# Narrowing stages: operand sums on VectorE in place, two pairs of k at a time, instead of GpSimd

## The chip, the cores and the metric

One core of one Trainium2 chip. The time is that of one execution of the program on the device, in microseconds (us), and a kernel's time is the median of its runs.

## What is computed

The reference runs two transformer blocks over a sequence of 512 tokens of width 1024 in fp32. Three times it ends a layer with a feed-forward network whose hidden width is 2816: a wide product, a gate, and a narrow product back to 1024 columns. The change touches only this last product.

```python
def swiglu(x, w_gate, w_up, w_down):
    return (jax.nn.silu(x @ w_gate) * (x @ w_up)) @ w_down

def _conv_ffn(x, w_in, conv_w, conv_b, w_out):
    u = x @ w_in
    up = jnp.pad(u, ((0, 0), (CONV_WIDTH_2 - 1, 0), (0, 0)))
    u = sum(conv_w[j] * up[:, j:j + s] for j in range(CONV_WIDTH_2)) + conv_b
    g, val = u[..., :D_FF_2], u[..., D_FF_2:]
    return (jax.nn.silu(g) * val) @ w_out
```

## The kernel before

An fp32 product is made of three TensorE products of rounded parts: ScalarE rounds an operand to its high part (`hh` of an activation, `wh` of a weight), VectorE subtracts to get the low part (`hl`, `wl`, line 185), and `mm3` (lines 436 to 438) multiplies high by high, high by low and low by high. Every weight piece that TensorE uses thus needs one VectorE subtraction of 1024 elements, and every activation operand one of 512.

The hidden activations lie in `hT`, 128 partitions by 22 k by 512 tokens. `down` makes the narrow product with seven block products in place of eight (a Strassen-like scheme): token halves `t` and `u`, pairs of k (`a1 = hT[:, 2g]`, `a2 = hT[:, 2g+1]`, eleven g), and halves of the columns. It has three stages, one after the other on TensorE:

- Stage 1 (`fetch1`, `pair`): four products per g into the banks R, Q, W, V, of `a1` (with its half u replaced by a1u - a2u, line 821) and `a2`. At its end R, Q, W and V are added to the residual `X` on VectorE (`end1` to `end4`: line 975 in block 1, line 1016 in the two convolution layers, then line 848).
- Stage 2 (`fetch2`): two products per g, of the sums that line 908 (VectorE) and line 909 (GpSimd, through `pool`, so the profile shows line 176) write into `hT`.
- Stage 3 (`third`): one product, of `s3 + s2`, which line 932 makes on GpSimd (again line 176), for two g at once, except the first.

In the profile's names an addition `hT<-hT` on GpSimd is one of line 909 (128x256) or of line 932 (128x512). The same queue of GpSimd also holds `biases`, line 422: four additions of a row to two tiles of `X`, 128x1024, which come once in each of the two convolution layers, and the multiplication `hT<-hT,tv` of `conv_ffn`, the last of the wide stage. `gains`, line 411, is VectorE's multiplication of `X` by a row. The layers are called layer 0 (`block1_ffn`), layer 1 (`conv_ffn(0)`) and layer 2 (`conv_ffn(1)`, the end of the program).

TensorE's order is written by hand. On the other engines a scheduler sets the order when the program is built; weight conversions run ahead of TensorE by a few pieces, and the sums of stages 2 and 3 are placed well ahead of use, most of them inside stage 1. Each engine then executes its own list strictly in order.

Of the kernel before, what the change touches and what calls it, by code (L numbers as in the profile page):

```python
# [16 lines left out]
ALU = mybir.AluOpType  # L17
# [5 lines left out]
S = 512  # L23
# [4 lines left out]
NF = D_FF // P  # L28
# [44 lines left out]
class Half:  # L73
# [6 lines left out]
    def fetch(self, j):  # L80
        if j in self.ops:
            return
        if j % 2 == 0:
            pc = self.net.piece()
            for e in range(2):
                c = slice(e * 512, (e + 1) * 512)
                self.pieces[j + e] = (pc[0][:, c], pc[1][:, c])
        self.ops[j] = self.lhs(self.order[j])
# [11 lines left out]
class Net:  # L100
# [699 lines left out]
    def operand(self, src, negative=False):  # L800

        self.operands += 1
        hp = self.hp[0 if self.operands % 8 in (1, 2) else 1]
        h = hp.tile([P, S], F32R, name="hh", tag="hh")
        l = hp.tile([P, S], F32R, name="hl", tag="hl")
        w = math.prod(src.shape[1:])
        view = lambda x: x[:, :w] if len(src.shape) == 2 else x[:, :w].rearrange("p (a b) -> p a b", b=256)
        if negative:
            self.nc.scalar.activation(view(h), src, AF.Copy, scale=-1.0)
            last = self.nc.vector.scalar_tensor_tensor(view(l), src, -1.0, view(h).bitcast(F32), op0=ALU.mult, op1=ALU.subtract)  # L810
        else:
            _, last = self.split(view(h), view(l), src)
        if 12 < self.operands <= 12 + NT:
            self.gains(last)
        return h, l
# [8 lines left out]
    def down(self, es, hT, first, done, last=False):  # L824

        nc, G = self.nc, NF // 2
        self.hp.append(es.enter_context(self.tc.tile_pool(name="hp", bufs=6, reuse_waits="tile")))
        t, u = slice(0, 256), slice(256, 512)  # L830
        TT = nc.vector.tensor_tensor
        bank = lambda pool, tag: [pool.tile([P, 512], F32, name="dn", tag=tag) for _ in range(2)]
        R, W, Q, V = bank(self.wk, "wk"), bank(self.wk, "wk"), bank(self.acc, "acc"), bank(self.acc, "acc")
        on = dict(skip_group_check=True)
        operand = self.operand

        def mms(ps, a, ca, b, cb, start, stop, tiles=(0, 1), **kw):

            for i in tiles:
                c, d = slice(256 * ca + i * P, 256 * ca + i * P + P), slice(512 * cb, 512 * cb + 512)  # L840
                self.mm3(ps[i], (a[0][:, c], a[1][:, c]), (b[0][:, d], b[1][:, d]), start, stop, **kw)

        def add(i, half, ps, op=ALU.add, begin=False):
            x = self.X[:, i, 512 * half:512 * half + 512]
            if begin:
                first(x, ps, op)
            else:
                TT(x, x, ps, op=op)  # L848

        def run(fetch, products, tail, wait=False):  # L850


            ops = []
            for g in range(G):
                while len(ops) < min(G, g + 1 + FETCH):
                    ops.append(fetch(len(ops)))
                if g < G - tail:
                    for f in products:
                        if wait and f is products[-1] and g < 2:
                            if g:  # L860
                                f(0, *ops[0])
                                f(1, *ops[1])
                        else:
                            f(g, *ops[g])
            for f in products:
                for g in range(G - tail, G):
                    f(g, *ops[g])
                f(None)

        def product(ps, a, ca, b, cb, begin, then):  # L870
            kw = {} if begin else on
            def f(g, *ops):
                if g is None:
                    then()
                else:
                    mms(ps, ops[a], ca, ops[b], cb, begin and g == 0, g == G - 1, **kw)
            return f


        def fetch1(g):  # L880
            if g + 1 < G:
                self.ahead.append(self.pair(hT, g + 1))
            return *self.ahead.pop(0), self.piece(), self.piece()

        def end1():
            for i in (0, 1):
                add(i, 0, R[i], begin=True)

        def end2():
            for i in (0, 1):  # L890
                add(i, 0, W[i])

        def end3():
            for i in (0, 1):
                add(2 + i, 1, Q[i], begin=True)

        def end4():
            for i in (0, 1):
                add(2 + i, 0, V[i], begin=True)

        self.boost = 0
        run(fetch1, [product(R, 0, 0, 2, 0, True, end1), product(Q, 0, 1, 3, 0, True, end3),
                     product(W, 1, 0, 2, 1, True, end2), product(V, 1, 1, 3, 1, True, end4)], 1, True)


        def fetch2(g):
            a1, a2 = hT[:, 2 * g, :], hT[:, 2 * g + 1, :]
            TT(a1[:, u], a1[:, u], a1[:, t], op=ALU.subtract)  # L908
            self.pool(a1[:, t], a2[:, t], a1[:, u], op=ALU.add)
            return operand(a1), self.piece()  # L910

        def end5():
            for i in (0, 1):
                add(i, 1, R[i], ALU.subtract, True)

        def end6():
            for i in (0, 1):
                add(i, 1, Q[i])
                done(i)

        self.pinned.enter_context(self.tc.manual_schedule(engines={mybir.EngineType.PE}))
        self.biases()
        run(fetch2, [product(R, 0, 1, 1, 0, False, end5), product(Q, 0, 0, 1, 1, False, end6)], 2)


        ops, tail = {}, 8 if last else 5

        def third(g):
            if g not in ops:
                m = 2 if g else 1  # L930
                s2, s3 = hT[:, 2 * g:2 * g + 2 * m:2, u], hT[:, 2 * g + 1:2 * g + 2 * m:2, u]
                self.pool(s3, s3, s2, op=ALU.add)
                x, w = operand(s3, True), self.piece()
                ops.update({g + e: (x, e, w, e) for e in range(m)})
            return ops[g]

        for g in range(G - tail):
            mms(R, *third(g), False, False, **on)
        for g in range(G - tail, G):
            third(g)  # L940
        if not last:
            self.new_xt()
        for i in (0, 1):
            if self.turns:
                self.turn(n=1)
            for g in range(G - tail, G):
                mms(R, *ops[g], False, g == G - 1, (i,), **on)
            for half in (0, 1):
                add(2 + i, half, R[i], (ALU.add, ALU.subtract)[half])
            done(2 + i)  # L950
# [609 lines left out]
```

## Time and profile before

| what | value |
|---|---|
| time, median of 3 runs (lowest to highest) | 1791.72 us (1788.81 to 1791.89) |
| time of the profiled execution | 1794.33 us |
| its span, first to last instruction | 1792.4 us |
| TensorE clock granted, mean | 0.975 of full speed |
| busy share: TensorE matmul, VectorE, ScalarE, GpSimd | 94%, 81%, 56%, 47% |

The rows further down come from the profiled execution, whose time is 2.6 us above the median of the runs. A busy share is a mean over the whole program; what counts here is which engine waits in the three narrowing stages, about 417 to 526 us, 1040 to 1160 us and 1664 to 1790 us.

### The profile page before, as it was taken

How to read it: one execution, taken by the hardware profiler on the slowest of the kernel's cores; microseconds unless marked ns; L12 is line 12 of the kernel's file. 1: busy time of each engine (PE TensorE's matmuls, PEld its weight loads, DVE VectorE, ACT ScalarE, POOL GpSimd, SP SyncE). 2: the span in 40 equal slices, each digit the busy share in tenths (PEclk: the TensorE clock that was granted, in tenths of full speed). 3: DMA queues.
4: the chain of work that ended last, by engine and by line, in shares of the span. 5: the costliest groups of instructions: out<-in, count | busy, mean ns of one | idle time of the engine just before them, and what ended most of it. 6: DMA issues, size and time to landing. Idle time of an engine off the chain costs nothing. (4 is left out here: it accounts for less than half of the span.)

```text
span 1792.4 us, 28144 instructions
## 1 busy us (share of the span) xinstructions
PE 1680.9 (94%) x10432; PEld 1490.2 (83%) x10432; DVE 1446.4 (81%) x2177; ACT 1008.8 (56%) x1733; POOL 850.0 (47%) x588
## 2 busy tenths in 40 slices
PE   7978999999999899999999997999998999999987
PEld 6856999998777788878999985887776889999865
DVE  6984676778885788977998899855888679888998
ACT  6663344545553587745665563644667555665652
POOL 2484733334235465217555546244232175655761
PEclk9988999999999999999999998999999999999998
DMA  6469566668876665744576688697442336666643
GB/s 230 168 187 254 158 152 193 176 190 308 319 223 174 162 165 146 202 108 137 162 192 176 183 297 292 197 243 190 115 119 81 99 108 158 188 173 185 202 153 112
DMA packets 106072, 326.05 MB, mean 182 GB/s; under 512 B 9888, under 2 KB 10016, under 8 KB 93904
## 3 DMA queue, kind: packets, MB, share of 16 engines
q1 hardware_dynamic: 73088, 215.53, 35.3%
q0 software_dynamic: 25648, 73.54, 21.8%
q10 hardware_dynamic: 7200, 35.20, 5.5%
q8 instruction: 82, 1.34, 0.3%
q14 instruction: 54, 0.44, 0.1%
HBM read 274.91 MB, written 73.43 MB: 194 GB/s over the span
## 5 line engine op out<-in xcount | busy, mean ns | idle before, releaser
L183 ACT ACTIVATE wh<-raw 128x1024 fp32r<-128x1024 f32 x457 | 450.6, 997 | 406.9 <-PE c L437 93.9
L185 DVE TENSOR_TENSOR wl<-raw,wh 128x1024 fp32r<-128x1024 f32 (+1 forms) x415 | 536.9, 1309 | 145.9 <-ACT wh L183 141.8
L176 POOL TENSOR_TENSOR raw<-raw 128x512 f32<-128x512 f32 x124 | 188.0, 1516 | 254.5 <-DMA raw<-raw 205.9
L436 PE MATMUL c<-xh,wh 128*128 128x256 f32 x992 | 284.4, 287 | 11.4 <-ACT m L519 10.3
L437 PE MATMUL c<-xl,wh 128*128 128x256 f32 x992 | 283.0, 285 | 0.0
L438 PE MATMUL c<-xh,wl 128*128 128x256 f32 x992 | 282.2, 284 | 0.0
L436 PEld LDWEIGHTS c<-xh,wh 128*128 128x128 f32 x992 | 191.0, 193 | 14.1 <-ACT m L519 12.4
L438 PE MATMUL dn<-wh,hl 128*128 128x512 f32 x462 | 182.0, 395 | 13.1 <-DVE hl L185 13.1
L437 PE MATMUL dn<-wl,hh 128*128 128x512 f32 x462 | 183.5, 398 | 9.0 <-DVE wl L185 8.9
L437 PEld LDWEIGHTS c<-xl,wh 128*128 128x128 f32 x992 | 191.2, 193 | 0.1
L438 PEld LDWEIGHTS c<-xh,wl 128*128 128x128 f32 x992 | 191.2, 193 | 0.0
L176 POOL TENSOR_TENSOR hT<-hT 128x256 f32<-128x256 f32 (+2 forms) x66 | 151.3, 2317 | 68.1 <-DVE hT L908 68.0
L436 PE MATMUL dn<-wh,hh 128*128 128x512 f32 x462 | 180.0, 395 | 0.0
L176 POOL TENSOR_TENSOR wl<-raw,wh 128x1024 fp32r<-128x1024 f32 (+1 forms) x42 | 95.8, 2286 | 87.0 <-ACT wh L183 83.0
L436 PE MATMUL fa<-xh,wh 128*128 128x256 f32 (+1 forms) x400 | 133.2, 333 | 1.7 <-ACT wh L183 1.7
L437 PE MATMUL fa<-xl,wh 128*128 128x256 f32 (+1 forms) x400 | 132.7, 332 | 1.1 <-DVE xl L185 1.1
L438 PE MATMUL fa<-xh,wl 128*128 128x256 f32 (+1 forms) x400 | 132.7, 332 | 0.8 <-DVE rs_t L326 0.8
L176 POOL TENSOR_TENSOR rs_r<-rs_t,mhalf 128x1 f32<-128x1 f32 (+1 forms) x40 | 32.4, 810 | 189.8 <-DVE rs_t L326 188.2
L437 PEld LDWEIGHTS dn<-wl,hh 128*128 128x128 f32 x462 | 88.1, 191 | 33.8 <-DVE wl L185 15.7
L438 PEld LDWEIGHTS dn<-wh,hl 128*128 128x128 f32 x462 | 88.1, 191 | 32.0 <-DVE hl L185 13.9
L150 POOL COPY paced<-wh 128x1 f32<-128x1 f32 x48 | 38.3, 798 | 154.3 <-ACT wh L183 154.1
L436 PEld LDWEIGHTS dn<-wh,hh 128*128 128x128 f32 x462 | 88.0, 191 | 18.4
(303 smaller groups left out, 4618.6 us busy)
## 6 DMA issues: line engine op xcount, KB each, us to landing
raw<-in_w_conv_dram SPq DMA_DIRECT2D x36, 1024.0 KB, 4.9
mixed<-in_narrow_dram ACTq DMA_DIRECT2D x48, 704.0 KB, 6.2
raw<-raw POOLq DMA_DIRECT2D x62, 512.0 KB, 5.1
raw<-mixed SPq DMA_DIRECT2D x51, 512.0 KB, 6.1
raw<-in_narrow_dram SPq DMA_DIRECT2D x48, 512.0 KB, 4.9
raw<-in_w_ffn_dram SPq DMA_DIRECT2D x18, 1024.0 KB, 4.9
mixed<-in_narrow_dram POOLq DMA_DIRECT2D x24, 704.0 KB, 10.1
mixed<-mixed POOLq DMA_DIRECT2D x24, 704.0 KB, 10.2
```

Source lines behind the costliest of these rows:

```text
L150: paced = self.nc.gpsimd.tensor_copy(m, self.ready[-1][0][:, 0:1].bitcast(F32))
L176: self.pooled = self.nc.gpsimd.tensor_tensor(*args, **kw)
L183: self.copied = self.nc.scalar.activation(hi, src, AF.Copy)
L185: return self.copied, sub(lo, src, hi.bitcast(F32), op=ALU.subtract)
L436: mm(ps, lh, rh, start=first, stop=False)
L437: mm(ps, lh, rl, start=False, stop=False)
L438: mm(ps, ll, rh, start=False, stop=last)
```

## The change

The 17 GpSimd additions of a layer go to VectorE. `fetch2` works on every second call only, for two pairs of k together: one subtraction and one addition of 128x2x256, and the addition is now written over `a2` half t, where before it was written over `a1` half t. The operand is then a contiguous run of 512 that begins in the middle of `a1`, so that its two halves change places, and the two products swap the number of the half that they read. `third` keeps its shape and changes engine.

```diff
+        flat = hT.rearrange("p k s -> p (k s)")
+
         def fetch2(g):
-            a1, a2 = hT[:, 2 * g, :], hT[:, 2 * g + 1, :]
-            TT(a1[:, u], a1[:, u], a1[:, t], op=ALU.subtract)
-            self.pool(a1[:, t], a2[:, t], a1[:, u], op=ALU.add)
-            return operand(a1), self.piece()
+            if g % 2 == 0:
+                a1, a2 = (hT[:, 2 * g + e:min(2 * g + 4, NF):2, :] for e in range(2))
+                TT(a1[:, :, u], a1[:, :, u], a1[:, :, t], op=ALU.subtract)
+                TT(a2[:, :, t], a2[:, :, t], a1[:, :, u], op=ALU.add)
+            return operand(flat[:, 2 * g * S + 256:2 * g * S + 768]), self.piece()
...
-        run(fetch2, [product(R, 0, 1, 1, 0, False, end5), product(Q, 0, 0, 1, 1, False, end6)], 2)
+        run(fetch2, [product(R, 0, 0, 1, 0, False, end5), product(Q, 0, 1, 1, 1, False, end6)], 2)
...
-                self.pool(s3, s3, s2, op=ALU.add)
+                TT(s3, s3, s2, op=ALU.add)
```

In the changed kernel the lines behind the diff have moved by three: 908 is 911, 909 is 912, 932 is 935, and 1016 is 1019.

GpSimd's list in layer 1, from the last multiplications of the wide stage to the three later additions of `biases` (line 422); before (-) there are sums of `hT` in between:

```order
+L176 TENSOR_TENSOR hT<-hT,tv 128x512 x3
 L422 TENSOR_TENSOR X<-X,row 128x2x512
-L176 TENSOR_TENSOR hT<-hT 128x256
-L176 TENSOR_TENSOR hT<-hT 128x2x256
-L176 TENSOR_TENSOR hT<-hT 128x256 x2
-L176 TENSOR_TENSOR hT<-hT 128x2x256
-L176 TENSOR_TENSOR hT<-hT 128x256 x2
-L176 TENSOR_TENSOR hT<-hT 128x2x256
 L319 DMA row<-in_rows_dram 128x1024
 L422 TENSOR_TENSOR X<-X,row 128x2x512 x3
```

Nothing of the sums is left on GpSimd, and the three additions of line 422 have only the row's load ahead of them.

VectorE's list in layer 1 where stage 1 ends and `X` is updated, before the change:

```order
L185 TENSOR_TENSOR wl<-raw,wh 128x1024
L1016 SCALAR_TENSOR_TENSOR X<-X,dn 128x512 x4
L185 TENSOR_TENSOR wl<-raw,wh 128x1024 x2
L848 TENSOR_TENSOR X<-X,dn 128x512 x2
L1016 SCALAR_TENSOR_TENSOR X<-X,dn 128x512 x2
L185 TENSOR_TENSOR hl<-hT,hh 128x512
```

The same place after it, with the last sums of the stage ahead of it:

```order
L912 TENSOR_TENSOR hT<-hT 128x2x256
L911 TENSOR_TENSOR hT<-hT 128x256
L935 TENSOR_TENSOR hT<-hT 128x2x256
L912 TENSOR_TENSOR hT<-hT 128x256
L185 TENSOR_TENSOR wl<-raw,wh 128x1024
L1019 SCALAR_TENSOR_TENSOR X<-X,dn 128x512 x3
L185 TENSOR_TENSOR wl<-raw,wh 128x1024 x2
L1019 SCALAR_TENSOR_TENSOR X<-X,dn 128x512
L848 TENSOR_TENSOR X<-X,dn 128x512 x2
L1019 SCALAR_TENSOR_TENSOR X<-X,dn 128x512 x2
L185 TENSOR_TENSOR hl<-hT,hh 128x512
```

The first operand of stage 2 (`hl`) still stands behind all eight instructions on `X`; the fourth of line 1016 has moved behind two weight conversions.

VectorE's list in layer 2 in the middle of stage 2, a piece of the difference:

```order
+L185 TENSOR_TENSOR hl<-hT,hh 128x512
 L810 SCALAR_TENSOR_TENSOR hl<-hT,hh 128x256
+L935 TENSOR_TENSOR hT<-hT 128x2x256
+L185 TENSOR_TENSOR wl<-raw,wh 128x1024
 L810 SCALAR_TENSOR_TENSOR hl<-hT,hh 128x512
+L935 TENSOR_TENSOR hT<-hT 128x2x256 x2
+L185 TENSOR_TENSOR wl<-raw,wh 128x1024
+L810 SCALAR_TENSOR_TENSOR hl<-hT,hh 128x512 x2
+L935 TENSOR_TENSOR hT<-hT 128x2x256
+L185 TENSOR_TENSOR wl<-raw,wh 128x1024
+L935 TENSOR_TENSOR hT<-hT 128x2x256
```

In layer 2 five of the six sums of stage 3 and one narrow one of stage 2 now come between the operands of stages 2 and 3, behind the end of stage 1.

## Rows read from the trace of the kernel before

**Rows 1.** The page's busy times: busy us, share of the span, instructions.

```profile
PE 1680.9 (94%) x10432; PEld 1490.2 (83%) x10432; DVE 1446.4 (81%) x2177; ACT 1008.8 (56%) x1733; POOL 850.0 (47%) x588
```

**Rows 2.** Busy time by stretch: stage 1 of layers 1, 2; then transition, stages 2-3.

```profile
core 0: us, PE busy (x) PEld busy (x) DVE busy (x) ACT busy (x) POOL busy (x), PEclk, DMA share, GB/s
1040.00:1104.00 64.00, 61.32 (x265) 49.01 (x265) 62.16 (x74) 36.36 (x47) 37.63 (x18) 1.00 0.91 317
1104.00:1120.00 16.00, 5.77 (x16) 4.25 (x15) 15.23 (x12) 2.37 (x4) 10.59 (x7) 0.68 0.69 246
1664.00:1730.00 66.00, 59.91 (x248) 46.77 (x247) 65.86 (x74) 36.84 (x49) 47.03 (x19) 0.97 0.51 167
1730.00:1779.00 49.00, 48.74 (x213) 39.38 (x212) 47.88 (x56) 22.26 (x27) 16.43 (x8) 1.00 0.40 134
```

**Rows 3.** Waits of TensorE, layers 0, 1, 2: us in total, times, longest.

```profile
PE dn L438 <- DVE hl L185: 2.9, 1, 2.9
...
PE dn L438 <- DVE hl L185: 10.2, 1, 10.2
PE dn L437 <- DVE wl L185: 2.5, 3, 1.9
...
PE dn L437 <- DVE wl L185: 6.4, 8, 2.1
```

**Rows 4.** Timeline, layer 1, end of stage 1: start, us, instruction [idle before, releaser].

```profile
1099.22 2.73 DVE L1016 SCALAR_TENSOR_TENSOR X<-X,dn 128x512 f32<-128x512 f32 x4 [1.84 <-PE dn L438]
1101.86 3.50 DVE L185 TENSOR_TENSOR wl<-raw,wh 128x1024 fp32r<-128x1024 f32 x2
...
1107.07 6.94 POOL L422 TENSOR_TENSOR X<-X,row 128x1024 f32<-128x1024 f32 x3
...
1107.67 6.90 DVE L185 TENSOR_TENSOR hl<-hT,hh 128x512 fp32r<-128x512 f32 x1
...
1114.62 0.79 PE L438 MATMUL dn<-wh,hl 128*128 128x512 f32 x1 [10.23 <-DVE hl L185]
```

**Rows 5.** VectorE by shape, 1664 to 1730: count | busy us, mean ns | idle.

```profile
L185 DVE TENSOR_TENSOR wl<-raw,wh 128x1024 fp32r<-128x1024 f32 x21 | 30.0, 1440 | 0.1
L185 DVE TENSOR_TENSOR hl<-hT,hh 128x512 fp32r<-128x512 f32 x25 | 23.0, 938 | 0.0
L411 DVE TENSOR_TENSOR X<-X,row 128x1024 f32<-128x1024 f32 x4 | 6.5, 1624 | 0.0
L821 DVE TENSOR_TENSOR hT<-hT 128x256 f32<-128x256 f32 x9 | 4.7, 534 | 0.0
```

**Rows 6.** The same in layer 1, 1040 to 1104.

```profile
L185 DVE TENSOR_TENSOR wl<-raw,wh 128x1024 fp32r<-128x1024 f32 x22 | 32.4, 1489 | 0.0
L185 DVE TENSOR_TENSOR hl<-hT,hh 128x512 fp32r<-128x512 f32 x20 | 15.8, 816 | 0.0
```

**Rows 7.** The same in layer 0, 482 to 500, with no sum on GpSimd.

```profile
L185 DVE TENSOR_TENSOR wl<-raw,wh 128x1024 fp32r<-128x1024 f32 x7 | 8.6, 1224 | 3.4 <-ACT wh L183 3.4
L185 DVE TENSOR_TENSOR hl<-hT,hh 128x512 fp32r<-128x512 f32 x10 | 6.5, 684 | 0.0
```

**Rows 8.** Timeline, layer 1, VectorE and GpSimd together.

```profile
1086.33 1.29 DVE L185 TENSOR_TENSOR hl<-hT,hh 128x512 fp32r<-128x512 f32 x2
1087.54 0.41 DVE L908 TENSOR_TENSOR hT<-hT 128x256 f32<-128x256 f32 x1
1087.87 1.22 DVE L185 TENSOR_TENSOR wl<-raw,wh 128x1024 fp32r<-128x1024 f32 x1
...
1086.55 19.94 POOL L176 TENSOR_TENSOR hT<-hT 128x256 f32<-128x256 f32 x8 [9.12 <-DVE hT L908]
```

**Rows 9.** Timeline, layer 2: GpSimd's first row, then VectorE's waits.

```profile
1669.70 5.16 POOL L176 TENSOR_TENSOR hT<-hT,tv 128x512 f32<-128x512 f32 x1 [4.58 <-ACT hh L183]
...
1652.41 1.23 DVE L185 TENSOR_TENSOR wl<-raw,wh 128x1024 fp32r<-128x1024 f32 x1 [1.93 <-ACT wh L183]
...
1763.75 0.69 DVE L848 TENSOR_TENSOR X<-X,dn 128x512 f32<-128x512 f32 x1 [0.89 <-PE dn L438]
```

**Rows 10.** The chain that ended last: its first row, and the last on VectorE.

```profile
1771.30 3.40 DVE X L383 x2
...
1787.69 0.75 DVE X L384
```

## The prediction

> **What bounds the kernel now.** I read the page's busy shares first, then the busy times of the narrowing stages, then what TensorE waits for there, then the durations of VectorE's instructions by shape, and last the timelines at the longest waits. TensorE is busy 94% of the span and VectorE 81% [rows 1], so the share alone says TensorE. By stage it reads otherwise: in stage 1 of layer 2 VectorE is busy 65.9 of 66 us while TensorE works 59.9, and in stage 1 of layer 1 it is 62.2 of 64 [rows 2]. All waits of TensorE in these stages are for VectorE, for `wl` or `hl`: 2.9 us in layer 0, 12.7 in layer 1, 6.4 in layer 2 [rows 3]. That is 22.0 us, the most that a faster supply of operands can take out of the waits themselves.
>
> VectorE is slow there because GpSimd stands in its way. With no sum on GpSimd `wl` takes 1224 ns and `hl` 684 [rows 7]; in layer 2 they mean 1440 and 938 [rows 5], in layer 1 1489 and 816 [rows 6]. The longest single wait shows the mechanism: an `hl` of 684 ns lasts 6.90 us, just as long as three additions of line 422 run on GpSimd, and TensorE idles 10.2 us for it [rows 4]. Both have two inputs in SBUF. An addition of line 422 takes 2.31 us there (6.94/3), and VectorE does nothing meanwhile. From 1652.4 us VectorE has no wait but 0.89 us until the end [rows 9], and the chain that ended last is VectorE's from 1771 to the end [rows 10]. So in layer 2 VectorE's work sets the end, in layer 1 TensorE waits at the end of stage 1, and in layer 0 TensorE loses 2.9 us once.
>
> The blocking isn't one-sided. From 1086.6 to 1106.4 eight sums on GpSimd take 19.94 us, while `hl` and `wl` beside them run at 1.29 for two and 1.22 [rows 8]: here GpSimd waited and VectorE paid nothing. The Trainium skill ("SBUF — State Buffer", Who interferes with whom) says that whichever of the two starts first has the shared pair for the whole instruction and the other fully blocks; the 6.90 us agree, but by the rule alone VectorE would pay for most sums. If it paid for all, at half of line 422's 2.31 us for a 512 and a quarter for a 256, a layer's 6 and 11 sums would hold it 13.3 us, and layer 2 would gain 13.3 - 6.7 + 0.9 = 7.5 us in place of the 4.3 worked out below. I use the stretch of the rows.
>
> **The change, part by part.**
>
> Removed from VectorE: eleven subtractions of line 908 a layer. One takes 0.33 us from its start to the next [rows 8], so 3.7 us.
>
> Added to VectorE: in each of lines 911, 912 and 935 five additions of 512 elements and one of 256, so 15 and 3. The trace has no 2x256 addition on VectorE; the nearest row is `hl`, 128x512, two of which take 1.29 us, so 0.60 each when the next overlaps its end, and 0.68 alone [rows 7, 8]. Line 912 reads what 911 has just written, so I take 0.68 for its five, 0.60 for the other ten, 0.33 for the three narrow ones: 3.4 + 6.0 + 1.0 = 10.4 us. The net is +6.7 us a layer. Ends: 10.0 if all overlap, 11.2 if none do.
>
> Given back to VectorE: the stretch. In layer 2 against the undisturbed times (1224 ns standing for the 1024-wide line 411 too) [rows 5, 7, 8]: `wl` 21 x 0.216 = 4.5, `hl` 25 x 0.254 = 6.4, line 411 4 x 0.40 = 1.6, line 821 9 x 0.12 = 1.1, together 13.6 us. Not all of it is the sums': one line 422 (2.3 us) and the long multiplication `hT<-hT,tv` (5.16 us mostly waiting [rows 9]; as a 512, half of a line 422, about 1.2) stay. 10.1 us go. In layer 1 [rows 6, 7]: 22 x 0.265 + 20 x 0.132 = 8.5 us, less the same 3.5, so 5.0. In layer 0 TensorE doesn't wait inside stage 1, so nothing there counts.
>
> On the path, layer by layer:
>
> *Layer 2.* VectorE is the bound from end to end, so its work counts: 6.7 - 10.1 = -3.4 us, and the added sums fill its idle 0.9 us at 1763.8 [rows 9], so **-4.3**. TensorE can follow: its 6.4 us of waits and the half-speed clock after them (0.97 mean over 66 us [rows 2], some 2 us) leave it 8. The order matters here: 5 of the wide sums stand behind the end of stage 1 and delay the final normalization, which is why TensorE's 8 us are not the gain.
>
> *Layer 1.* Up to the end of stage 1 VectorE gets 5.8 net (10 subtractions go; 912 five wide, 911 five, 935 three, and three narrow: 3.4 + 4.8 + 1.0 - 3.4) and 5.0 back; its wait of 1.84 for TensorE [rows 4] covers the rest. Of the 2.5 us of waits for `wl` half should go, because the stretch lies ahead of line 422 and many of the sums behind it: **-1.2**. Then the 10.2 us. GpSimd's list before holds the eight sums of rows 8 until 1106.4, so line 422 began at 1107.07; its first input is ready when the fourth line 1016 ends. In the new order that is after three of them, two `wl` of 1.2 without the stretch that makes them 3.50 now, and one more: 1099.2 + 1.9 + 2.3 + 0.7 = 1104.1. The `hl` behind it still waits for all three additions, and TensorE for it, but 2.9 us sooner: **-2.9**. Should `hl` slip in between the first and second addition, the second `hl` meets the others, so the gain stays near 3 to 4 us.
>
> *Layer 0.* The 2.9 us wait is an `hl` that stands behind eight additions to `X` which wait for TensorE; that order stays: **0**.
>
> The sum is -4.3 - 1.2 - 2.9 = -8.4 us. The profiled execution would go from 1794.3 to 1785.9; against the median of the runs, 2.6 us below it, 1791.7 - 8.4 = **1783 us**.
>
> Nothing new waits for ScalarE: each sum on VectorE stands behind the `hl` of the same pair, which had already waited for ScalarE's read. GpSimd loses 17 sums a layer; it idles.
>
> **The rivals.**
>
> *The relief is larger (0.09).* If the `hl` after stage 1 of layer 1 misses line 422 altogether, the 10.2 us wait falls to what layer 0 has, 2.9, and the 2 us at half clock behind it (0.68 over 16 us [rows 2]) shrink too. For it: GpSimd starts earlier. Against: three additions of 2.31 us still follow the same update of `X`. With it -8.4 - 6 = 1777; with all of layer 1's waits gone 1772.
>
> *No change (0.21).* VectorE's relief equals its new work: at 11.2 us for the sums and the stretch given back only two thirds (6.7 in layer 2), layer 2 gains nothing, and layer 1 gives 0 to 3: 1788 to 1794, about 1790. For it: rows 8, where sums cost VectorE nothing, so that its stretch may be owed to other work on GpSimd.
>
> *Slower (0.13).* VectorE, which had no gap in layer 2, now has 6.7 us more to do, and line 422 on GpSimd, freed of the sums ahead of it, comes earlier and takes the port at a moment when TensorE has no operand in hand. The point where it decides is in layer 2: if less than 5.8 of the 10.1 us come back (6.7 less the idle 0.9), it is longer than before. At a quarter back, layer 2 costs 6.7 - 2.5 - 0.9 = +3.3, and in layer 1 5.8 - 1.3 - 1.8 = +2.7 more wait ahead of line 422: +6, 1798. Against it: the stretch in rows 5 is measured, and GpSimd has nothing else there. A rule speaks for it: the Trainium skill ("Perfetto Trace Analysis", Optimizing Scalar/DVE Operations) advises to move work to GpSimd where VectorE is saturated, and adds that the shared read port may undo it; the second half is what rows 4 to 6 show.
>
> **How the numbers follow.** My forecast has 0.57, the larger relief 0.09, no change 0.21, slower 0.13. The likeliest case by itself is 1778 to 1788: the sums between 10.0 and 11.2 a layer, the stretch of layer 2 between 8 and 13.6, the transition between 0 and 4 us. Runs of this kernel lie within 3 us of each other, so 0.2% (3.6 us) is about what can be told from no change. Faster by more than that takes in the first two cases, 0.66; within it 0.21; slower 0.13. The range reaches up to cover no change and down to the larger relief: 1773 to 1793 leaves out about the slow case and the tail of the other.
>
> **What would show it.** Right: no `hT<-hT` of 128x256 or 128x512 on GpSimd; lines 911, 912 and 935 near 0.68 us for 512 elements; `wl` in stage 1 of layer 2 near 1.28 us and `hl` near 0.75; the waits of TensorE for `wl` in layer 2 down from 6.4 us to under 2; the long wait of layer 1 ending within about 12 us of the end of R's products instead of 15. Wrong: `wl` and `hl` as long as before, so GpSimd's sums were not what stretched them; a new wait of TensorE before 1104 us in layer 1 as long as the old; or, in layer 2, TensorE freed but the final normalization as late as before, which would say that the sums placed behind stage 1 took everything back.

## The result and the profile after

The changed kernel takes 1782.1 us (median of 4 executions, 1780.6 to 1783.6) where the kernel before took 1791.8 beside it: a ratio of 0.9937, 95% interval 0.9921 to 0.9953. With more executions on another chip it was 0.9950 (0.9931 to 0.9969). The prediction was 1783.0.

The busy times of the page after, in the columns of [rows 1]:

```profile
PE 1673.8 (94%) x10432; PEld 1485.5 (83%) x10432; DVE 1445.4 (81%) x2198; ACT 1008.7 (57%) x1733; POOL 779.9 (44%) x537
```

VectorE's total is the same within 1 us of [rows 1], though it makes all the sums now; GpSimd's is 70 us less. The busy times by stretch, which answer to the second and third row of [rows 2] (the second stretch, like that of before, ends 0.9 us ahead of the first update of `X`; the first begins 0.9 us ahead of it, where that of before began 4.8 behind it):

```profile
1097.00:1113.00 16.00, 11.58 (x39) 8.51 (x38) 15.08 (x13) 6.83 (x9) 11.30 (x6) 0.79 0.81 312
1649.00:1715.00 66.00, 65.07 (x313) 54.50 (x314) 65.95 (x89) 42.82 (x60) 23.54 (x4) 1.00 0.62 205
```

In 66 us of stage 1 of layer 2 TensorE now works 65.1 us instead of 59.9, at a granted clock of 1.00, which is the 2.4 GHz level, instead of a mean of 0.97. In the 16 us of layer 1's transition it works 11.6 instead of 5.8, and 11.4 in the 16 us that begin 4.8 us behind the first update. VectorE is as full as before in both. TensorE's waits in layers 1 (two rows) and 2 (one), against [rows 3]:

```profile
PE dn L438 <- DVE hl L185: 4.6, 2, 4.0
PE dn L437 <- DVE wl L185: 0.5, 1, 0.5
...
PE dn L437 <- DVE wl L185: 1.9, 3, 1.0
```

With the 3.0 of layer 0, which stayed, 22.0 us of waits are now 10.0. VectorE's durations by shape in layer 2, 1649 to 1715, against [rows 5]:

```profile
L185 DVE TENSOR_TENSOR wl<-raw,wh 128x1024 fp32r<-128x1024 f32 x23 | 31.1, 1365 | 0.0
L185 DVE TENSOR_TENSOR hl<-hT,hh 128x512 fp32r<-128x512 f32 x25 | 16.3, 678 | 0.0
L411 DVE TENSOR_TENSOR X<-X,row 128x1024 f32<-128x1024 f32 x4 | 4.8, 1211 | 0.0
L821 DVE TENSOR_TENSOR hT<-hT 128x256 f32<-128x256 f32 x10 | 4.0, 410 | 0.0
L911 DVE TENSOR_TENSOR hT<-hT 128x512 f32<-128x512 f32 x5 | 3.4, 678 | 0.0
L912 DVE TENSOR_TENSOR hT<-hT 128x512 f32<-128x512 f32 x5 | 3.4, 677 | 0.0
```

`hl`, line 411 and line 821 are back at their undisturbed 0.68, 1.21 and 0.41 us. `wl` is not (1365 against 1224): one line 422 and one long multiplication `hT<-hT,tv` still fall on it. A wide sum takes 0.68 us. Last the timeline of the transition of layer 1, which answers to [rows 4]:

```profile
1102.76 1.28 DVE L848 TENSOR_TENSOR X<-X,dn 128x512 f32<-128x512 f32 x2
...
1103.95 1.27 DVE L1019 SCALAR_TENSOR_TENSOR X<-X,dn 128x512 f32<-128x512 f32 x2
1104.12 8.43 POOL L422 TENSOR_TENSOR X<-X,row 128x1024 f32<-128x1024 f32 x3 [3.63 <-DVE X L848]
1105.15 1.87 DVE L185 TENSOR_TENSOR hl<-hT,hh 128x512 fp32r<-128x512 f32 x1
1106.94 3.38 DVE L185 TENSOR_TENSOR wl<-raw,wh 128x1024 fp32r<-128x1024 f32 x1
...
1107.07 0.80 PE L438 MATMUL dn<-wh,hl 128*128 128x512 f32 x1 [3.98 <-DVE hl L185]
```

GpSimd had waited 3.63 us for the last line 848 and started its three additions the moment that ended. Before, `hl` stood still for all three; here it lasts 1.87 us and is done 0.6 us after the first addition. Then `wl` loses 2.2 us to the second. The two engines take turns, and TensorE resumes at 1107.1 instead of 1114.6.

**Where the time came from.** I cut the profiled executions at three rows of VectorE in layers 1 and 2: the first subtraction of line 821, the first update of `X` behind R's products, and the end of the last line 384. They give four stretches, in us.

| kernel | layer 1, stage 1 | then to layer 2 | layer 2, stage 1 | then to the end |
|---|---|---|---|---|
| before | 75.2 | 548.2 | 83.5 | 58.2 |
| after | 72.1 | 543.0 | 75.0 | 60.4 |
| after, once more | 72.1 | 543.7 | 75.0 | 60.4 |

Layer 1 gave 3.1 and 5.2 us, layer 2 gave 8.5 and took 2.1 back. The second profile of the changed kernel repeats each stretch within 0.7 us, where whole executions scatter by some 7 us to either side. The second stretch is the least sure: it also holds attention and the wide stage of layer 2, which no edit here touches, and that part alone lasts from 480.2 to 484.7 us over the profiles of this document. So the lengths of layer 1 below run from the first subtraction of line 821 only to the end of the layer's last product into `dn`: 140.6 us before and 132.7 in both profiles after, a gain of 7.9, of which 3.1 are stage 1 and 4.7 what follows. Layer 0 gave nothing: its first update of `X` is at 472.88 before and 473.03 after. So layers 1 and 2 gave 7.9 and 6.4, together 14.2 us before rounding; the medians differ by 9 to 10. The profiled execution of before was 2.6 us above its median, and between layers 0 and 1 the one after lost 1.8 us, without a cause that I could name; of that stretch the profiles below show anything from 2.7 us less to 4.7 more than before.

### The profile page after: what moved, and what is told of

Same layout as the page of the kernel before. It is cut to its first block, busy times and chain, and to the rows that moved or that the text cites. A ratio compares the mean times of both kernels' runs of the same rounds, so it can differ in the third digit from the quotient of the medians.

```text
span 1779.6 us, 28078 instructions
## 1 busy us (share of the span) xinstructions
PE 1673.8 (94%) x10432; PEld 1485.5 (83%) x10432; DVE 1445.4 (81%) x2198; ACT 1008.7 (57%) x1733; POOL 779.9 (44%) x537
## 5 line engine op out<-in xcount | busy, mean ns | idle before, releaser
L436 PE MATMUL c<-xh,wh 128*128 128x256 f32 x992 | 284.2, 287 | 13.3 <-ACT m L519 9.0
L436 PE MATMUL fa<-xh,wh 128*128 128x256 f32 (+1 forms) x400 | 133.4, 333 | 1.6 <-ACT wh L183 1.6
L176 POOL TENSOR_TENSOR hT<-hT,tv 128x512 f32<-128x512 f32 x44 | 93.2, 2117 | 37.5 <-DVE tv L1004 33.2
```

Source lines behind the costliest of these rows:

```text
L176: self.pooled = self.nc.gpsimd.tensor_tensor(*args, **kw)
L436: mm(ps, lh, rh, start=first, stop=False)
```

## The experiments

My theory: sums on GpSimd shut VectorE out while they read, and VectorE is what layer 2 lasts; in layer 1 they also hold back line 422. The rivals: the pairs of k and the new order are the gain; or only the queue ahead of line 422. Ratios are to the kernel before, on the same chip.

**Sums on GpSimd that nobody needs.** The orders of the other engines stay.

```diff
...
+            nc.gpsimd.tensor_tensor(spare[:, 0], hT[:, 2 * g, t], hT[:, 2 * g + 1, t], op=ALU.add)
             return operand(flat[:, 2 * g * S + 256:2 * g * S + 768]), self.piece()
...
                 TT(s3, s3, s2, op=ALU.add)
+                nc.gpsimd.tensor_tensor(spare[:, :m], s3, s3, op=ALU.add)
```

> The changed kernel, and in addition GpSimd makes 17 sums a layer of the sizes it made before, read from hT and written to a spare tile that nobody reads; the orders of TensorE, VectorE and ScalarE stay as they are. My theory (GpSimd's reads of two SBUF inputs stretch VectorE): VectorE keeps its 6.7 us of new work a layer and loses what it was given back, about 10 us in layer 2 and 5 in layer 1, so wl in stage 1 of layer 2 goes from 1365 ns back over 1440 and the time from 1782 to 1794 to 1800 us. Rival A (the gain is the order of the work and the pairs, not the engine's reads): 1782 us, within 1.5. Rival B (only the place of line 422 behind the sums counted): the three additions of line 422 in layer 1 start late again, TensorE's wait there goes back toward 10 us, layer 2 stays: 1786 to 1789.

Measured: 1.0048 (1.0030 to 1.0066), 1802.2 us where the kernel before took 1794.0 beside it: 18 to 20 us more than the changed kernel by the ratios, a little more than my theory had. Rival A is out, since order and pairs were the changed kernel's, and B is, since layer 2 got longer too. The busy times of the two stretches of layer 2, with the columns of [rows 2], in three kernels, a fence each: before, after, and with the spare sums:

```profile
1647.37:1730.86 83.49, 76.31 (x375) 62.47 (x374) 81.38 (x98) 48.12 (x66) 56.35 (x23) 0.98 0.53 178
1730.86:1789.10 58.24, 48.23 (x210) 38.69 (x208) 56.98 (x74) 21.95 (x27) 18.41 (x10) 0.94 0.37 130
```

```profile
1640.88:1715.88 75.00, 73.40 (x378) 62.27 (x377) 73.01 (x99) 48.02 (x66) 28.67 (x6) 1.00 0.61 207
1715.88:1776.24 60.36, 48.35 (x207) 37.98 (x205) 60.13 (x80) 21.86 (x26) 18.91 (x10) 0.93 0.33 115
```

```profile
1648.05:1725.21 77.16, 73.64 (x377) 62.19 (x377) 75.19 (x98) 48.00 (x66) 47.36 (x11) 1.00 0.60 201
1725.21:1791.99 66.78, 50.65 (x207) 38.97 (x205) 66.55 (x80) 21.83 (x26) 33.88 (x23) 0.93 0.30 104
```

The third busy time is VectorE's. With the spare sums it is busy 141.7 us in layer 2 instead of 133.1, with the same instructions, and the layer is 8.6 us longer: every microsecond that VectorE lost there is in the time. Layer 1 takes 140.3 us, 7.6 more, where I had 5. One sign failed: `wl` means 1390 ns in the 66 us that end 0.9 ahead of layer 2's first update of `X` (1365 in the changed kernel), not 1440 or more; 6.4 of the 8.6 us came behind that stage.

**Copies in their place.** Of one piece of `hT`, so one input instead of two.

```diff
...
+            nc.gpsimd.tensor_copy(spare[:, 0], hT[:, 2 * g + 1, t])
...
+                nc.gpsimd.tensor_copy(spare[:, :m], s3)
```

> As the run with spare sums, but GpSimd copies one piece of hT (one input) where that one adds two. If two inputs of SBUF are what shuts VectorE out, VectorE's durations stay at those of the changed kernel and the time at 1782 to 1785 us, and what it loses against the changed kernel is only that line 422 is queued behind the copies. If any work of GpSimd on SBUF does it, it comes out like the spare sums, 1794 or more.

Measured: 0.9982 (0.9966 to 0.9998). In layer 2 the copies cost VectorE 1.3 us (134.5 busy) where the sums cost 8.6. But a copy is also shorter: one of 128x256 takes 0.39 us at its shortest, a spare sum 0.73. And it does shut VectorE out. Here is `hl`, 0.68 us when undisturbed, beside a spare sum and beside a copy, a fence each:

```profile
1688.02 1.22 DVE L185 TENSOR_TENSOR hl<-hT,hh 128x512 fp32r<-128x512 f32 x1
```

```profile
1687.23 0.88 DVE L185 TENSOR_TENSOR hl<-hT,hh 128x512 fp32r<-128x512 f32 x1
```

A sum costs it 0.54 us, a copy 0.20. So one input in place of two doesn't end the blocking; it makes it shorter, and the run doesn't show whether two inputs are needed for anything more. The kernel is still 6 to 8 us slower than the changed one by the ratios, and this is where:

```profile
1101.97 4.17 POOL L938 COPY spare<-hT 128x256 f32<-128x256 f32 x4
...
1104.84 1.27 DVE L848 TENSOR_TENSOR X<-X,dn 128x512 f32<-128x512 f32 x2
...
1106.73 6.93 POOL L422 TENSOR_TENSOR X<-X,row 128x1024 f32<-128x1024 f32 x3
1107.23 6.99 DVE L185 TENSOR_TENSOR hl<-hT,hh 128x512 fp32r<-128x512 f32 x1
...
1114.28 0.79 PE L438 MATMUL dn<-wh,hl 128*128 128x512 f32 x1 [9.50 <-DVE hl L185]
```

The copies and the row's load kept GpSimd busy past the end of line 848 at 1106.1. Line 422 started 0.6 us later, ran without a pause, and `hl` stood still for all three additions and took 6.99 us, as in [rows 4]. TensorE resumes 14.6 us after the first update of `X` instead of 9.2. So the sums had two effects, and this run has little but the second: a queue ahead of line 422.

**The additions back on GpSimd, with the pairs.**

```diff
-                TT(a2[:, :, t], a2[:, :, t], a1[:, :, u], op=ALU.add)
+                self.pool(a2[:, :, t], a2[:, :, t], a1[:, :, u], op=ALU.add)
...
-                TT(s3, s3, s2, op=ALU.add)
+                self.pool(s3, s3, s2, op=ALU.add)
```

> The changed kernel's pairs of k and its in-place sums, but the additions of lines 912 and 935 on GpSimd; VectorE keeps the subtractions of line 911, five wide and one narrow. My theory: these subtractions cost VectorE as much as the eleven narrow ones before (5 x 0.68 + 0.33 = 3.7 us), GpSimd adds as many elements as before, so the time is that of the kernel before, 1789 to 1793 us, and TensorE's waits in layers 1 and 2 sum to about 20 us. Rival (the pairs and the place of the sums are the gain): 1782 to 1785.

Measured: 1.0013 (0.9997 to 1.0029), the kernel before; the rival is out. TensorE's waits are 10.5 us in layer 1 and 7.8 in layer 2. VectorE by shape in stage 1 of layer 2 is stretched as in [rows 5]:

```profile
L185 DVE TENSOR_TENSOR wl<-raw,wh 128x1024 fp32r<-128x1024 f32 x20 | 29.7, 1498 | 2.0 <-ACT wh L183 1.9
L185 DVE TENSOR_TENSOR hl<-hT,hh 128x512 fp32r<-128x512 f32 x19 | 16.4, 883 | 0.4 <-ACT hh L183 0.4
```

**One stage at a time.** The changed kernel with line 935 on GpSimd again:

```diff
-                TT(s3, s3, s2, op=ALU.add)
+                self.pool(s3, s3, s2, op=ALU.add)
```

> The changed kernel with the sums of stage 3 (line 935) back on GpSimd: 6 of the 12 wide-and-narrow additions of a layer move, half of the elements. My theory: half of the stretch comes back (5 us in layer 2, 2.5 in layer 1) for half of the new work, 3.4 us, and nothing is added behind the end of stage 1: 1785 to 1788 us, about half of the gain. Rival (the gain is layer 1's transition, which turns on line 422 having nothing ahead of it): the sums of stage 3 stand ahead of line 422 again and it comes out at 1789 or more. Rival (only the sums of stage 2 did harm, since those of stage 3 mostly ran behind the end of stage 1): 1780 to 1783, as good as the whole change or better.

And the kernel before with line 932 on VectorE:

```diff
-                self.pool(s3, s3, s2, op=ALU.add)
+                TT(s3, s3, s2, op=ALU.add)
```

> The kernel before, with only the sums of stage 3 (line 932) moved to VectorE; stage 2 stays one pair at a time with its additions on GpSimd. It is the other half of the run with stage 2 alone, which gained 0.3% of the whole change's 0.6%. My theory (each GpSimd sum costs VectorE a stretch, and the costs add): the rest, 0.2 to 0.4% under the kernel before, with about 5 us out of the stretch of layer 2's stage 1 and 2 us given back behind it. Rival (only when all sums are gone does line 422 find GpSimd waiting and VectorE in front): no gain in layer 1, so at most 0.15%.

Measured: 0.9968 (0.9952 to 0.9985) with stage 2 alone, about the half that I expected, and 0.9995 (0.9977 to 1.0013) with stage 3 alone, where I had 0.2 to 0.4% less than before. Layer 2 lasts 138.4 and 139.8 us against 141.7 before and 135.4 after, so the halves give 3.3 and 1.9 of the 6.4 us there. Layer 1 doesn't split so: in both profiles GpSimd was waiting when line 422 became free to run, it took turns with `hl`, and the layer lasted 135.1 and 135.8 us, 5.5 and 4.8 of the 7.9. For stage 3 alone the whole executions don't show the 6.7 us that the layers of its profile do; that execution took 1789.9 us, 3.3 less than the median of its kind. GpSimd waited only 1.8 us for line 848 in it, against 3.6 in the changed kernel, so it may miss the turn in other executions; that is a guess.

**Line 422 on VectorE.**

```diff
-            self.nc.gpsimd.tensor_tensor(x, x, r[:, c].unsqueeze(1).to_broadcast([P, 2, 512]), op=ALU.add)
+            self.nc.vector.tensor_tensor(x, x, r[:, c].unsqueeze(1).to_broadcast([P, 2, 512]), op=ALU.add)
```

> The changed kernel with the four additions of line 422 on VectorE, so that GpSimd has nothing left that shuts VectorE out in the narrowing stages but the multiplications before them. VectorE gets 4 x 1.22 = 4.9 us a layer more and is no longer shut out for 2.3 us at each: layer 2 about 2 us better, layer 1 about as before, since three of the four now stand ahead of the first hl (3.7 us): 1779 to 1784 us, 0.4 to 0.7% under the kernel before. Rival (line 422 is what the rest of the stretch is): 4 us or more better than the changed kernel, 0.85% or more.

Measured: 0.9969 (0.9952 to 0.9985), by the ratios 0.2 to 0.3% worse than the changed kernel, which I had not expected. Stage 1 of layer 2 is 2.3 us shorter, and what follows 4.6 longer:

```profile
1728.94 3.49 DVE L422 TENSOR_TENSOR X<-X,row 128x1024 f32<-128x1024 f32 x3
1732.35 4.62 DVE L185 TENSOR_TENSOR wl<-raw,wh 128x1024 fp32r<-128x1024 f32 x4
...
1764.85 2.89 POOL L376 TENSOR_TENSOR X<-X,row 128x1024 f32<-128x1024 f32 x1 [0.23 <-ACT X L375]
1767.82 2.67 POOL L377 TENSOR_TENSOR X<-X,row 128x1024 f32<-128x1024 f32 x1
1768.21 4.49 DVE L185 TENSOR_TENSOR wl<-raw,wh 128x1024 fp32r<-128x1024 f32 x2
1771.62 0.79 PE L437 MATMUL dn<-wl,hh 128*128 128x512 f32 x1 [6.42 <-DVE wl L185]
```

Behind the updates of `X` the three additions now stand ahead of the weights. TensorE waits 7.9 us for `wl` in layer 2, but only 1.5 of them there. The other 6.4 come late: GpSimd still makes a multiplication and an addition of the final normalization (lines 376 and 377), which I had left out of account, and here they run while VectorE's last two `wl` are still to be made, so that these take 4.49 us. In the changed kernel the last `wl` had begun before them, and the two fell on VectorE's own normalization. In layer 1 the first `hl` stands behind the three additions, TensorE waits 6.2 us for it instead of 4.0, and the layer lasts 134.1 us. Not everything gains by leaving GpSimd.

**The first operands of stage 2 ahead of the updates of `X`,** in the changed kernel and, with the same edit, in the one before.

```diff
-                    ops.append(fetch(len(ops)))
+                    with ExitStack() as up:
+                        if not wait and len(ops) < 2:
+                            up.enter_context(self.tc.high_priority(offset=250))
+                        ops.append(fetch(len(ops)))
```

> The changed kernel, with the first two operands of stage 2 of each layer put ahead of the updates of X at the end of stage 1, so that no hl stands behind line 422. What is left of TensorE's waits for hl after the change (3.0 us in layer 0, 4.6 in layer 1) should go, with the slower clock that follows them: 4 to 7 us faster than the changed kernel, 0.85 to 1.0% under the kernel before. Rival (the wait only changes its name: TensorE then waits for the updates of X that free its banks, or for the weights behind line 422): within 0.1% of the changed kernel.

> The kernel before with the same early operands and all its sums on GpSimd: what the end of stage 1 of layers 0 and 1 is worth without touching the sums. TensorE has two operands of about 2.6 us of work each in hand while line 422 shuts VectorE out for 6.9 us, so the 10.2 us wait of layer 1 should fall to 2 to 4 and the 2.9 of layer 0 should go: 8 to 11 us with the clock, 0.45 to 0.6% under the kernel before. Layer 2 stays stretched (wl near 1440 ns, hl near 940). Rival (the wait moves to the next operand that line 422 shuts out): under 0.2%.

Measured: 0.9934 (0.9911 to 0.9957), the changed kernel's time, as the rival had it. And 0.9984 (0.9966 to 1.0001) for the kernel before, less than the 0.45 to 0.6% that I expected and not clear of no change; in its profile layer 1 lasts 136.0 us, 4.6 less than before with all sums still on GpSimd, and layer 2 gains nothing. In the first, layer 0's wait fell from 3.0 us to 1.9, now for an update of `X`, and in layer 1 the wait came back under another operand:

```profile
1105.71 6.98 POOL L422 TENSOR_TENSOR X<-X,row 128x1024 f32<-128x1024 f32 x3
1106.45 6.53 DVE L915 TENSOR_TENSOR hT<-hT 128x256 f32<-128x256 f32 x1
...
1114.24 0.80 PE L438 MATMUL dn<-wh,hl 128*128 128x512 f32 x1 [7.12 <-DVE hl L185]
```

Line 422 came 0.4 us late here, behind the load of its row, and shut out a sum of 0.41 us (line 915 is 912 here) for 6.5; the third `hl` stood behind it.

**Line 422 held back,** by a copy of one column of a low part that must be there first: of the second operand of stage 2 in the changed kernel, and of the fourth in the one with early operands.

```diff
...
+            if g == 1 and self.owed:
+                held = nc.gpsimd.tensor_copy(self.held, x[1][:, :1].bitcast(F32))
+                with self.tc.issue_after(held.ins):
+                    self.rows_on(*self.owed)
...
```

(`self.owed` names the three later additions of line 422, and `rows_on` makes them.)

> The changed kernel, with the last three additions of line 422 held on GpSimd by a one-column copy of the second low part of stage 2, so that they start about 3.5 us later; VectorE's order is the same. My theory (what line 422 costs is when it shuts VectorE out): the first hl is made right behind the updates of X, and TensorE's wait for it falls from 4.0 to about 2.9 us, as in layer 0; then the three additions run back to back, as they do where they were ready before, and shut VectorE out for up to 6.9 us while TensorE has two operands of 2.6 us of work: a wait of 1 to 3 us there. In sum 0 to 2 us either way against the changed kernel. Rival (with the first operand out of the way the port costs nothing more): 3 us or more better than the changed kernel.

> The early operands of the run above and line 422 held behind the fourth low part of stage 2. In the run with early operands alone TensorE waited 7.1 us in layer 1, because sums and the third hl stood behind the three additions. My theory: with four operands made ahead of line 422, TensorE has work while VectorE is shut out, and that wait falls to 2 us or less: 4 to 6 us better than the changed kernel, 0.87 to 1.0% under the kernel before. Rival (VectorE is the bound through the stage, and what it loses to line 422 comes out later in any case): within 0.15% of the changed kernel.

Measured: 0.9957 (0.9940 to 0.9973) and 0.9937 (0.9920 to 0.9955); the changed kernel beside them, 0.9950. The timeline of the first (its line 438 is 442, its 422 is 426):

```profile
1106.26 0.68 DVE L185 TENSOR_TENSOR hl<-hT,hh 128x512 fp32r<-128x512 f32 x1
1107.00 0.68 PE L442 MATMUL dn<-wh,hl 128*128 128x512 f32 x1 [2.79 <-DVE hl L185]
...
1108.75 1.11 POOL L920 COPY held<-hl 128x1 f32<-128x1 f32 x1 [7.16 <-DVE hl L185]
1109.83 7.55 POOL L426 TENSOR_TENSOR X<-X,row 128x1024 f32<-128x1024 f32 x3
...
1112.87 2.27 DVE L185 TENSOR_TENSOR hl<-hT,hh 128x512 fp32r<-128x512 f32 x1
```

`hl` takes its 0.68 us and the wait for it is 2.8, as expected; two later ones of 0.8 and 2.1 us come in its place, and layer 1 lasts 134.5 us against 132.7, within the 2 us that I had. In the second the wait of 7.1 us is down to two of 1.0 and 2.0, but near the end of the layer TensorE (the transposes of line 337) now waits for another low part of VectorE's:

```profile
PE pt L337 <- DVE xl L185: 2.6, 1, 2.6
```

The layer lasts 132.3 us, as in the changed kernel within 0.4. So what these waits give back comes out elsewhere, as the rival of that run had it. What sets the length of layer 1 stays open: I took it to be VectorE's own work, which no run took away, but from 1114 to 1160 us of the changed kernel TensorE is busy 44.9 us of 46 and VectorE 40.5. No version beats the changed kernel by more than the intervals.

The changed kernel again, as the measure for these:

> The changed kernel once more, with more executions, as the measure for the runs beside it. Every theory: 0.6 to 0.7% under the kernel before; in layer 1 the three additions of line 422 start as the last update of line 848 ends, and the first hl gets in between the first and the second of them, so TensorE's wait is near 4 us and not near 10.

Measured: 0.9950 (0.9931 to 0.9969), a little less of a gain than I expected. Its profile repeats the transition: the first of the three additions starts 0.09 us behind the last line 848, and TensorE waits 4.0 us.

**One pair at a time.**

```diff
-            if g % 2 == 0:
-                a1, a2 = (hT[:, 2 * g + e:min(2 * g + 4, NF):2, :] for e in range(2))
-                TT(a1[:, :, u], a1[:, :, u], a1[:, :, t], op=ALU.subtract)
-                TT(a2[:, :, t], a2[:, :, t], a1[:, :, u], op=ALU.add)
+            a1, a2 = hT[:, 2 * g, :], hT[:, 2 * g + 1, :]
+            TT(a1[:, u], a1[:, u], a1[:, t], op=ALU.subtract)
+            TT(a2[:, t], a2[:, t], a1[:, u], op=ALU.add)
```

> The changed kernel with the sums of stage 2 on VectorE, in place, but for one pair of k in each call: 22 narrow sums a layer in place of 10 wide and 2 narrow. By the rows of before a narrow one takes 0.33 to 0.41 us and a wide one 0.60 to 0.68, so VectorE has 0 to 1.5 us a layer more to do: 1 to 3 us slower than the changed kernel, 0.5 to 0.6% under the kernel before. Rival (the pairs are what makes room on VectorE): 5 us or more slower than the changed kernel.

Measured: 0.9951 (0.9933 to 0.9969), the same as the changed kernel beside it. In the profiles layer 1 lasts 133.4 us and layer 2 136.4, against 132.7 and 135.4: together 1.7 us more, as expected. The engine is the change; the pairs are worth 1.7 us in these profiles, which whole executions don't show.

## Why the prediction was right

The total was 1 us off, and that closely by luck, since its terms were further off. The steps, one by one:

- *What bounds.* Right for layer 2, and the spare sums show it: 8.6 us more on VectorE, 8.6 us more in the layer.
- *The sums' cost, 10.4 us and 6.7 net.* Right. A wide sum is 0.68 us and mostly 0.60 from its start to the next, so 10.1 and 6.4. An overlap is lost, as I had it, where line 912 directly follows the 911 whose result it reads: 0.71 or 0.72 us from start to start. But the order built has that once in layer 1 and nowhere in layer 2; another instruction stands between.
- *The stretch, 10.1 us in layer 2.* A little small. VectorE's busy time in the two stretches of the layer went from 138.4 to 133.1; with 6.4 us of new work that is 11.6 us given back. VectorE's idle time fell by 1.1 us, where I had 0.9. Layer 2: 6.4 us gained for 4.3 forecast. The 3.5 us that I left for line 422 and the multiplications are there in stage 1, but all on `wl`, so `wl` came out above my 1.28 us and `hl` below my 0.75. The sums behind the end of stage 1 do delay the end, by 2.1 us.
- *The `wl` waits of layer 1, 1.2 us.* Too small: they fell from 2.5 us to 0.5 and stage 1 is 3.1 us shorter.
- *The transition of layer 1, 2.9 us.* Right in part: line 422 starts earlier and TensorE's wait ends earlier. That it starts at 1104.12, where I had 1104.1, is luck. The three additions don't wait for the fourth line 1016 (1019 after) but for the last line 848, as the `[3.63 <-DVE X L848]` after the change shows; that ended at 1106.55 before, so GpSimd's sums and the row's load made line 422 only 0.5 us late. Counted from the first update of `X`, it started 7.9 us behind before and 6.2 after, where my sum had 4.9. From that update to TensorE's return it takes 9.2 us instead of 15.4. The step that failed is "the `hl` behind it still waits for all three additions", and with it the price that I put on the other case, "the gain stays near 3 to 4 us". `hl` did slip in, and the second `hl` cost TensorE 0.6 us only, since by then TensorE had an operand to work on. The layer kept 4.7 us of the 6.2 at its last product.
- *Layer 0: nothing.* Right.

So the layers gave 14.2 us in the profiles where I had 8.4, and the medians 9 to 10. The total was nearer than its terms: layer 1 was too small by 4 us and layer 2 by 2, and about 5 us of the gain the medians don't show. The 3 us within which I took runs to lie came from three runs; 35 on another chip lie between 1787.2 and 1801.0.

The rule that I set against the trace, of the Trainium skill ("SBUF — State Buffer", Who interferes with whom), gave a gain of 7.5 us in layer 2 where the stretch of the rows gave 4.3; the measured 6.4 lies between them. My count was off there: a layer has 5 wide and 12 narrow sums on GpSimd, not 6 and 11, so the 13.3 us are 12.7 and the 7.5 are 6.9, nearer to the measured gain. I also took too much from [rows 8] against the rule: of the 19.94 us the first sum took 11.43, until VectorE had a gap at 1097.4, and of the others VectorE did pay, 3.50 us for two `wl` in [rows 4] instead of 2.4. The same section says that a VectorE instruction with at most one SBUF input, outside the 2-port perf modes, does not contend with GpSimd. The trace agrees: two of line 1019, which read `X` and a PSUM bank, take 1.27 us beside line 422, and two of line 848 just ahead of it 1.28.

## What to carry to other kernels

Work on GpSimd that reads SBUF is not free because GpSimd idles: where VectorE is full, price it by the stretch of VectorE's instructions beside it, shape by shape, against a stage without it, and compare that with the work's own time on VectorE. Here, in layer 2, the 17 sums cost VectorE 11.6 us from GpSimd and 6.4 net from its own queue. Look also at what stands behind such work in GpSimd's queue: in layer 1 a start about half a microsecond late went with a TensorE that came back 5 to 6 us later, though not every late start did (next section).

## What the hardware showed that I had not expected

At the transition of layer 1 line 422 either shut VectorE out whole or took turns with it. `hl`, `wl` or a sum is VectorE's first instruction there with two inputs in SBUF; the times are in us.

| kernels | first of three starts, us behind the last line 848 | three take | VectorE's first |
|---|---|---|---|
| after (twice), spare sums, stage 2 alone, stage 3 alone, one pair at a time, before with early operands | 0.08 to 0.10 | 8.43 to 8.45 | `hl`, 1.86 to 1.88 |
| before | 0.52 | 6.94 | `hl`, 6.90 |
| spare copies | 0.62 | 6.93 | `hl`, 6.99 |
| after with early operands | 0.37 | 6.98 | sum, 6.53 |
| pairs with the additions on GpSimd | 5.2 | 7.05 | `wl`, 8.25 |
| line 422 held; early operands and held | 4.7; 8.0 | 7.55; 7.53 | `hl`, 2.27; 1.65 |

In the first group GpSimd was waiting for line 848; in the next four rows its own queue held it up, and it kept VectorE out over three instructions in a row. But lateness alone doesn't decide it: in the two runs of the last row line 422 started 4.7 and 8.0 us behind, VectorE's `hl` came during the second addition, and it got in ahead of the third. In layer 2 the two took turns in every profile that has line 422 on GpSimd, also with spare sums ahead of it in the queue. The other way round, VectorE, running without a gap, kept GpSimd out for longer: one line 422 of 2.3 us, free to start at 1073.8, took 25.3 us in the changed kernel, while `hl` and `wl` beside it ran at their undisturbed lengths. Why the engine that holds the port passes it on in the one case and not in the other I could not settle.
